# Branch outputs loaded straight into the low operand and split there, another planner's price for linear matmuls, and a beginning without GpSimd

## The chip, the cores and the metric

One core of one Trainium2 chip runs the whole layer in one launch. The metric is the device time of one execution in microseconds (us), the median of several executions. The kernel before takes 1955.33 us (median of three, 1954.95 to 1957.14).

## What is computed

The reference is one layer of a decoder trunk on x of 1024 positions by 1024 channels, all in float32. The gains, biases and norms are inputs.

```python
h = rms_norm(x, norm_g)
proj = einsum('bsd,dn->bsn', h, w_in)            # 11 blocks of 1024 columns, 16 gate columns, 3 x 1024 merge columns
ya = conformer_conv(a_val, a_glu, ...) * silu(a_gate)   # GLU, causal depthwise conv of width 31, LayerNorm, swish
yb = hgrn2(b_q, b_f, b_i, ...) * silu(b_gate)           # gated linear recurrence, 8 heads of 128
yc = forgetting_attention(c_q, c_k, c_v, ...) * silu(c_gate)  # 16 heads of 64, forget bias on the logits
branch_d = einsum('bskc,kcd->bskd', stack([ya, yb, yc]), w_branch)
mixed = sum(sigmoid(merge) * branch_d, over the three branches)
out = x + einsum('bsd,de->bse', mixed, w_out)
```

## The kernel before, in words

Everything is held transposed: channels on the 128 partitions, the 1024 positions along the free axis, in two halves of 512. A linear product is a "job" of 128 output columns (`Job`). Because the tensor engine's float32 product is taken in a rounded form (`F32R`), each operand is split into a high part (the rounded copy, made by ScalarE) and a low part (what is left, a subtraction on VectorE), and a job adds three products: high by high, low by high, high by low. A job so has 2 halves x 8 channel blocks x 3 = 48 matmuls of 128x128 by 128x512, all issued from L112 (`sc.mm`). Job 0 is narrow (the 16 forget gates) and has two products, 32 matmuls. `hT` holds the normed input (`hT_hi`, `hT_lo`), `whi` and `wlo` the weights of a job.

**Order.** `lin` (L352) walks the list of jobs; the first three go through their first halves, then through their second (`seq`). Everything else (the attention `att` and `soft`, the recurrence `hgrn`, the convolution `conv`, the loads `yload`) is a coroutine. `Sched.run` decides when a coroutine's next piece is emitted: it keeps a planned clock for each engine and lets a piece go when its planned ready time has been passed by TensorE's planned clock. Each linear matmul moves that clock by the number of ns given to `sc.mm`, 216 in L370 to L373. VectorE's long convolution is held near TensorE's planned clock in the same way. The order of emission is the priority from which a list scheduler then makes the final, fixed order of each engine and of each DMA queue; `tc.high_priority(HP)` lifts the instructions inside it by 300 places, and `tc.keep_in_program_order` (`K`, `pin`) ties an instruction behind the one before it on its engine.

**Stages.** (1) The beginning, L1200 to L1326: the eight blocks of 128 rows of x are loaded, `ident` is built (`make_identity`, GpSimd), 16 products of `ident` with itself (`NWARM`, L1215) run, each block is squared and summed by ScalarE (`x_sq`), its inverse root is refined on VectorE, the block is multiplied with `norm_g` (spread over all partitions in `gbc`) on VectorE or GpSimd, and it is transposed into `hT` by TensorE. The first four blocks are scaled inside the transposing product (`dgs`, L1269), the last four before it (L1254, L1258). GpSimd also makes `wlo` of jobs 1 and 2. (2) Eight rounds over channel blocks with the jobs of branches c and b. (3) The convolution stage, in which VectorE carries 31 taps for each of eight blocks and TensorE the jobs of branch c's output; it begins with `yload("c")`. (4) Branch b's outputs (after `yload("b")`), the gates of branch a, and the merge. (5) The last product with `w_out`, straight to the output.

**`yload` (L953)** brings a branch's output back from DRAM: for each of the eight channel blocks it takes one of the shared buffers `fa` (`F.get`, after `need(1)`), loads 512 KB into it, lets ScalarE make `Y["hi"][k]` and VectorE `Y["lo"][k]`, and gives the buffer back. `Y["hi"]` and `Y["lo"]` lie where the buffers of stage 2 (`fb`, queries, keys, gates) lay, opened by `swap` (L1151). VectorE and ScalarE take these instructions at the place where they were emitted. The jobs of the branch wait for `Y[b]`.

**`masks` (L294)** makes constants of the recurrence, by GpSimd (`affine_select`) and 16 small copies on ScalarE (L319 to L322).

Of the kernel before, what the change touches and what calls it, by code (L numbers as in the profile page):

```python
# [19 lines left out]
P = 128  # L20
# [27 lines left out]
PAD = 96  # L48
# [151 lines left out]
def build(tc, x, norm_g, w_in, conv_w, conv_b, ln_g, ln_b, hgrn_g, f_bias, qn_g, kn_g,  # L200
# [40 lines left out]
    make_identity(nc, ident)  # L241
# [14 lines left out]
    ones64 = const.tile([P, 64], F32, name="ones64")  # L256
    nc.vector.memset(ones64, 1.0)
# [11 lines left out]
    dgs = [const.tile([P, P], F32, name=f"dg{i}") for i in range(2)]  # L269
# [24 lines left out]
    def masks():  # L294
# [22 lines left out]
        for r in range(4):  # L317
            a = slice(r * 32, r * 32 + 32)
            nc.scalar.activation(cm[0][a, 0:32], ident[a, r * 32:r * 32 + 32], AF.Copy)  # L319
            nc.scalar.activation(cm[0][a, 32:48], lvl1[a, r * 16:r * 16 + 16], AF.Copy)  # L320
            for m in (2, 8):
                nc.scalar.activation(cm[m][a, :], lvl[m][a, r * 48:r * 48 + 48], AF.Copy)  # L322
# [29 lines left out]
    def lin(jobs, hooks):  # L352
        seq = [(0, 0), (1, 0), (2, 0), (0, 1), (1, 1), (2, 1)]
        seq += [(n, h) for n in range(3, len(jobs)) for h in (0, 1)]
        for m, (n, half) in enumerate(seq):
# [12 lines left out]
            for k in range(KT):  # L368
                a, b = X[0][k][:, hs], X[1][k][:, hs]
                sc.mm(ps, j.hi[:, k, :], a, k == 0, False, 216)  # L370
                sc.mm(ps, j.hi[:, k, :], b, False, j.narrow and k == KT - 1, 216)
                if not j.narrow:
                    sc.mm(ps, j.lo[:, k, :], a, False, k == KT - 1, 216)  # L373
                if k == 3:
                    yield 0
            if m in hooks:
                hooks[m]()
# [233 lines left out]
    def soft(st, i, T, MB, blks):  # L611
# [44 lines left out]
        for h in range(2):  # L656
            sc.mm(po[h * 64:(h + 1) * 64, 256:512], ones64, M[:, h, :], True, True, 225)
# [563 lines left out]
    def x_sq(i, pin):
        pin(nc.scalar.activation(sq[:, 0:S], xts[i][:, 0:S], AF.Square, accum_out=ss[:, i, 0:1]))

    def x_sqrt(i, pin):
        v, r, _ = col3(i)
        pin(nc.vector.tensor_scalar(out=v, in0=v, scalar1=1.0 / S, scalar2=EPS, op0=ALU.mult,
                                    op1=ALU.add))
        pin(nc.scalar.activation(r, v, AF.Sqrt))

    def x_g(i, pin):  # L1230
        e = nc.gpsimd if i % 2 else nc.vector
        pin(e.tensor_tensor(out=xg[i][:, 0:S], in0=xts[i][:, 0:S], in1=gbc[:, 0:S], op=ALU.mult))

    def x_newton(i, pin):
        v, r, e = col3(i)
        pin(nc.vector.reciprocal(r, r))
        pin(nc.vector.scalar_tensor_tensor(out=e, in0=r, scalar=v, in1=r, op0=ALU.mult,  # L1237
                                           op1=ALU.mult))
        pin(nc.vector.tensor_scalar(out=e, in0=e, scalar1=-0.5, scalar2=1.5, op0=ALU.mult,
                                    op1=ALU.add))  # L1240

    def x_dg(i, pin):
        v, r, e = col3(i)
        x_newton(i, pin)
        pin(nc.vector.tensor_scalar(out=dgs[i % 2], in0=ident, scalar1=r, scalar2=e,
                                    op0=ALU.mult, op1=ALU.mult))

    def x_rows(i, pin):

        v, r, e = col3(i)  # L1250
        xt = xg[i][:, 0:S]
        x_newton(i, pin)
        if i % 2:
            pin(nc.vector.tensor_scalar(out=xt, in0=xt, scalar1=r, scalar2=e, op0=ALU.mult,  # L1254
                                        op1=ALU.mult))
        else:
            pin(nc.vector.tensor_tensor(out=r, in0=r, in1=e, op=ALU.mult))
            pin(nc.vector.scalar_tensor_tensor(out=xt, in0=xts[i][:, 0:S], scalar=r,  # L1258
                                               in1=gbc[:, 0:S], op0=ALU.mult, op1=ALU.mult))

    def x_mm(i, pin):
        for hb in range(2):
            sbanks.append(sbanks.pop(0))
            pt = pts[i, hb] = sbanks[-1]
            for q in range(4):
                kk = hb * 4 + q
                o, a = pt[:, q * P:(q + 1) * P], xg[i][:, kk * P:(kk + 1) * P]
                if i < 4:
# [19 lines left out]
    def free(ins):  # L1288
        return ins
# [78 lines left out]
```

## Time and profile before

| | us |
|---|---|
| median of 3 runs | 1955.33 (1954.95 to 1957.14) |
| the profiled execution, whole | 1956.24 |
| its span, first to last instruction | 1954.5 |
| TensorE busy in the span | 1910.3 (98%) |
| VectorE, ScalarE, GpSimd busy | 1285.0, 956.5, 194.8 |
| mean granted clock of TensorE | 0.993 of full speed |

How to read it: the span is cut into stretches, and in each one looks first at what TensorE lacks to being busy and at the granted clock (1.00 is the 2.4 GHz level, 0.50 the 1.2 GHz level). A TensorE that is "busy" at half clock is counted as busy, so both columns are wanted. Then the list of waits says whom TensorE waited for, and the timeline shows the instructions around such a wait.

### The profile page before, as it was taken

To read this page: it belongs to the slowest core of one execution; us is meant where nothing else is said; L and a number is where in the kernel's file an instruction comes from. 1 tells how busy PE (TensorE), PEld (TensorE's weight loads), DVE (VectorE), ACT (ScalarE), POOL (GpSimd) and SP (SyncE) were. 2 spreads that over 40 slices of the span, in tenths; PEclk is the share of its full clock that TensorE was granted. 3 is DMA by queue.
4 is the path that set the end of the run, shared out by engine and by line. 5 is a ranking of instruction groups with operands and counts; after the bars stand their busy time and mean duration, and the time that the engine had idled before them with its cause. 6 is when DMAs were issued, how large, how long until landed. Compare 5 with 4: busy or idle time off the path is not lost.

```text
span 1954.5 us, 27130 instructions
## 1 busy us (share of the span) xinstructions
PE 1910.3 (98%) x11112; PEld 1550.0 (79%) x11112; DVE 1285.0 (66%) x1689; ACT 956.5 (49%) x1524; POOL 194.8 (10%) x157
## 2 busy tenths in 40 slices
PE   6999999999999999999999979999999999999999
PEld 5777877878778787787877857888888888888888
DVE  5357675676756867658677999999993367513431
ACT  5666868768687686776875231111131234312210
POOL 4011120211201211012021100000000110000000
PEclk9999999999999999999999989999999999999999
DMA  4111111111111111111112142222354553212431
GB/s 144 43 33 45 44 33 55 44 44 41 36 45 54 33 37 52 44 47 30 44 44 66 33 129 76 76 65 76 97 167 146 164 174 110 81 54 87 129 121 52
DMA packets 173140, 141.35 MB, mean 72 GB/s; under 512 B 4917, under 2 KB 155445, under 8 KB 173016
## 3 DMA queue, kind: packets, MB, share of 16 engines
q1 hardware_dynamic: 173016, 139.62, 23.2%
q8 instruction: 87, 1.43, 0.3%
q14 instruction: 37, 0.30, 0.1%
HBM read 110.24 MB, written 29.36 MB: 71 GB/s over the span
## 4 chain that ended last, share of the span: by engine, by line
PE 88%; DVE 5%; ACT 3%; issue 2%; DMA 1%; POOL 0%; DVEq 0%; SPq 0%; ACTq 0%; POOLq 0%
PE bank L112 86%; DVE fa L133 3%; PE bank L116 1%; ACT fb L125 1%; DMA zdram<-fa 1%; ACT fa L125 1%; DVE fa L129 1%; DVE wlo L348 1%; DMA fa<-zdram 1%; ACT khi L125 0%; DVE ylo L129 0%; DVE fb L129 0%; ACT whi L347 0%; DVE ss L1237 0%; PE bank L1271 0%
## 5 line engine op out<-in xcount | busy, mean ns | idle before, releaser
L112 PE MATMUL bank<-hT_hi,whi 128*128 128x512 f32 x1792 | 709.2, 396 | 3.2 <-ACT fb L125 1.5
L112 PE MATMUL bank<-hT_hi,wlo 128*128 128x512 f32 x1792 | 704.9, 394 | 0.4 <-DVE wlo L348 0.4
L112 PE MATMUL bank<-hT_lo,whi 128*128 128x512 f32 x1792 | 702.9, 392 | 0.0
L112 PEld LDWEIGHTS bank<-hT_hi,whi 128*128 128x128 f32 x1792 | 337.7, 188 | 77.9 <-issue 7.2
L112 PEld LDWEIGHTS bank<-hT_hi,wlo 128*128 128x128 f32 x1792 | 337.4, 188 | 76.1 <-issue 7.4
L112 PEld LDWEIGHTS bank<-hT_lo,whi 128*128 128x128 f32 x1792 | 337.8, 188 | 68.1 <-issue 3.8
L347 ACT ACTIVATE whi<-wraw 128x1024 fp32r<-128x1024 f32 x137 | 145.1, 1059 | 348.8 <-PE bank L112 334.3
L129 DVE TENSOR_TENSOR fa<-fa,fa 128x512 f32<-128x512 f32 (+3 forms) x299 | 236.5, 807 | 104.2 <-ACT fa L125 54.0
L133 DVE SCALAR_TENSOR_TENSOR fa<-fa,taps,fa 128x1024 f32<-128x1024 f32 x240 | 297.5, 1277 | 1.2
L348 DVE TENSOR_TENSOR wlo<-wraw,whi 128x1024 fp32r<-128x1024 f32 x135 | 171.9, 1273 | 162.5 <-ACT whi L347 162.2
L125 ACT ACTIVATE fa<-bank 128x512 f32<-128x512 f32 (+1 forms) x175 | 98.0, 565 | 170.4 <-PE bank L112 147.3
L112 PE MATMUL bank<-yhi,whi 128*128 128x512 f32 x384 | 150.8, 397 | 7.7 <-ACT yhi L125 7.7
L112 PE MATMUL bank<-ylo,whi 128*128 128x512 f32 x384 | 151.5, 395 | 6.2 <-DVE ylo L129 6.2
L125 ACT ACTIVATE fb<-bank 128x512 f32<-128x512 f32 (+6 forms) x269 | 121.2, 463 | 63.3 <-PE bank L112 36.9
L112 PE MATMUL bank<-yhi,wlo 128*128 128x512 f32 x384 | 150.7, 393 | 0.0
L129 DVE TENSOR_TENSOR fb<-fb,fb 128x512 f32<-128x512 f32 (+5 forms) x122 | 87.5, 733 | 33.1 <-ACT fb L125 29.3
L125 ACT ACT_TABLE_LOAD x83 | 106.5, 1283 | 5.1 <-DVE fb L129 3.6
L125 ACT ACTIVATE fa<-fa 128x1024 f32<-128x1024 f32 (+3 forms) x95 | 87.9, 940 | 39.3 <-DMA zdram<-fa 27.6
L133 DVE SCALAR_TENSOR_TENSOR fa<-fa,bank 128x512 f32<-128x512 f32 x82 | 56.0, 682 | 75.7 <-PE bank L112 75.7
L125 ACT ACTIVATE fa<-bank,negF,rk 128x256 f32<-128x256 f32 (+1 forms) x176 | 84.3, 549 | 38.4 <-PE bank L112 38.4
L125 ACT ACTIVATE fb<-fb 128x256 f32<-128x256 f32 (+5 forms) x105 | 77.1, 743 | 51.9 <-DVE fb L129 47.8
L112 PEld LDWEIGHTS bank<-yhi,whi 128*128 128x128 f32 x384 | 72.9, 191 | 24.3 <-ACT yhi L125 9.6
(200 smaller groups left out, 2097.3 us busy)
## 6 DMA issues: line engine op xcount, KB each, us to landing
wraw<-in_w_in_dram SPq DMA_DIRECT2D x113, 512.0 KB, 3.8
wraw<-in_w_branch_dram SPq DMA_DIRECT2D x24, 512.0 KB, 3.8
zdram<-fa SPq DMA_DIRECT2D x16, 512.0 KB, 2.7
mdram<-fa SPq DMA_DIRECT2D x32, 256.0 KB, 2.0
fa<-mdram SPq DMA_DIRECT2D x16, 512.0 KB, 4.4
fa<-zdram SPq DMA_DIRECT2D x16, 512.0 KB, 4.3
fa<-in_x_dram SPq DMA_DIRECT2D x9, 512.0 KB, 6.9
yb<-fb SPq DMA_DIRECT2D x8, 512.0 KB, 2.9
```

What stands on the lines that cost most here:

```text
L112: self.nc.tensor.matmul(out, lhsT=lhsT, rhs=rhs, start=start, stop=stop)
L116: self.nc.tensor.transpose(out, in_, ident)
L125: return self.nc.scalar.activation(out, in_, func, **kw)
L129: self.nc.vector.tensor_tensor(out=out, in0=a, in1=b, op=op)
L133: self.nc.vector.scalar_tensor_tensor(out=out, in0=a, scalar=s, in1=b, op0=op0, op1=op1)
L347: pin(nc.scalar.activation(j.hi, j.raw, AF.Copy))
L348: pin(eng.tensor_tensor(out=j.lo, in0=j.raw, in1=j.hi.bitcast(F32), op=ALU.subtract))
```

## The change

`ident` is now made without GpSimd: VectorE counts 1 to 128 along the free axis (a scan over ones), a product with one row turns the count into a column, and a comparison gives the identity. `norm_g` is no longer spread over the partitions: its 8 x 128 values are loaded from ScalarE's queue, transposed, and applied as a per-partition scale while the transposed blocks are taken out of PSUM (`gcol`). All eight blocks are scaled in place by VectorE and transposed. The first four blocks fill eight banks, one per channel block, so that one instruction per channel block and engine takes 512 columns out; the second four follow after the first, with hooks inside jobs 1 and 2 of `lin`. All `wlo` are made by VectorE. The five small loads of `gq`, `gk` and `fb` go from the sync queue to ScalarE's. The 16 small copies in `masks` go from ScalarE to GpSimd. `yload` loads all eight blocks straight into `Y["lo"]`, with no shared buffer, and then, at raised priority, copies each to `Y["hi"]` and subtracts in place. The planner's price of a linear matmul is 228 ns.

```diff
-PAD = 96
+PAD = 32
...
-    make_identity(nc, ident)
+    num = const.tile([P, P], F32, name="num")
+    ones64 = const.tile([P, P], F32, name="ones64")
+    nc.vector.memset(ones64, 1.0)
+    nc.vector.tensor_tensor_scan(out=num, data0=ones64, data1=ones64, initial=0.0, op0=ALU.mult,
+                                 op1=ALU.add)
+    nc.tensor.matmul(banks[6][:, 0:1], lhsT=num[0:1, :], rhs=ones64[0:1, 0:1], start=True, stop=True)
+    row_t = const.tile([P, 1], F32, name="row_t")
+    nc.vector.tensor_copy(row_t, banks[6][:, 0:1])
+    nc.vector.tensor_scalar(out=ident, in0=num, scalar1=row_t, scalar2=None, op0=ALU.is_equal)
...
-            nc.scalar.activation(cm[0][a, 0:32], ident[a, r * 32:r * 32 + 32], AF.Copy)
+            nc.gpsimd.tensor_copy(cm[0][a, 0:32], ident[a, r * 32:r * 32 + 32])
...
-                sc.mm(ps, j.hi[:, k, :], a, k == 0, False, 216)
+                sc.mm(ps, j.hi[:, k, :], a, k == 0, False, 228)
...
+                if (m, k) in hooks:
+                    hooks[m, k]()
                 if k == 3:
                     yield 0
-            if m in hooks:
-                hooks[m]()
...
         for k in range(KT):
-            yield need(1)
-            t = F.get()
-            nc.sync.dma_start(out=t[:, 0:S], in_=ydram[b][k])
-            sc.act(Y["hi"][k], t[:, 0:S], AF.Copy)
-            sc.tt(Y["lo"][k], t[:, 0:S], Y["hi"][k].bitcast(F32), ALU.subtract)
-            fput(t)
+            nc.sync.dma_start(out=Y["lo"][k].bitcast(F32), in_=ydram[b][k])
+        for k in range(KT):
+            with tc.high_priority(HP):
+                sc.act(Y["hi"][k], Y["lo"][k].bitcast(F32), AF.Copy)
+                sc.tt(Y["lo"][k], Y["lo"][k].bitcast(F32), Y["hi"][k].bitcast(F32), ALU.subtract)
             yield 0
...
+    nc.scalar.dma_start(out=g8, in_=norm_g.rearrange("a (k p) -> (a k) p", p=P))
+    for h in range(2):
+        for dst, a in ((gq, qn_g), (gk, kn_g)):
+            nc.scalar.dma_start(out=dst[h * 64:(h + 1) * 64, :], in_=a[0].unsqueeze(1))
+    nc.scalar.dma_start(out=fb, in_=f_bias[0].unsqueeze(1))
     for i in range(KT):
         nc.sync.dma_start(out=xts[i][:, 0:S], in_=x[i * P:(i + 1) * P, :])
-        if i == 0:
-            nc.sync.dma_start(out=gbc[:, 0:S], in_=norm_g.broadcast_to([P, S]))
-        if i in (3, 5, 7):
-            fetch(jobs[(i - 3) // 2])
+        if i in (3, 4, 7):
+            fetch(jobs[{3: 0, 4: 1, 7: 2}[i]])
...
+    def x_sq(i):
+        v, r = ss[:, i, 0:1], ss[:, i, 1:2]
+        K(nc.scalar.activation(sq[:, 0:S], xts[i][:, 0:S], AF.Square, accum_out=v))
+        K(nc.vector.tensor_scalar(out=v, in0=v, scalar1=1.0 / S, scalar2=EPS, op0=ALU.mult,
+                                  op1=ALU.add))
+        K(nc.scalar.activation(r, v, AF.Sqrt))
+
+    def x_rows(i):
...
+        K(nc.vector.tensor_scalar(out=xt, in0=xt, scalar1=r, scalar2=e, op0=ALU.mult, op1=ALU.mult))
...
+    def x_out(bk, k, half, pin=lambda ins: ins):
+        dst = [h[:, k, half * H2:(half + 1) * H2] for h in hT]
+        pin(nc.scalar.activation(dst[0], bk, AF.Copy, scale=gcol[:, k:k + 1]))
+        pin(nc.vector.scalar_tensor_tensor(out=dst[1], in0=bk, scalar=gcol[:, k:k + 1],
+                                           in1=dst[0].bitcast(F32), op0=ALU.mult, op1=ALU.subtract))
+
+    for i in range(4):
+        x_sq(i)
+        if i:
+            x_rows(i - 1)
+    x_rows(3)
+    for i in range(4):
+        for k in range(KT):
+            x_tr(banks[k], k, i, 0)
+    split(jobs[0], nc.vector, K)
     for k in range(KT):
+        x_out(banks[k], k, 0, K)
+        if k == 3:
+            split(jobs[1], nc.vector, K)
+    def x_second():
+        for i in range(4, KT):
+            x_sq(i)
+            if i > 4:
+                x_rows(i - 1)
+        x_rows(KT - 1)
+        split(jobs[2], nc.vector, K)
+
+    def x_two_out(g):
+        bk = xbanks[:4]
+        for i in range(4, KT):
+            for k in range(4):
+                x_tr(bk[k], 4 * g + k, i, 1)
+        for k in range(4):
+            x_out(bk[k], 4 * g + k, 1)
...
-    sc.run(lin(jobs, {0: lambda: x_two_out(4), 1: lambda: x_two_out(6)}))
+    sc.run(lin(jobs, {(1, 7): lambda: x_two_out(0), (2, 3): lambda: x_two_out(1)}))
```

## Rows read from the trace of the kernel before

**Rows 1.** Busy time by stretch: length, busy us of each engine, TensorE clock, DMA

```profile
0.00:48.86 48.86, 29.55 (x172) 25.89 (x173) 28.20 (x70) 27.09 (x63) 21.12 (x29) 0.96 0.44 144
...
146.59:195.45 48.86, 47.32 (x458) 35.13 (x458) 38.61 (x74) 31.33 (x59) 8.56 (x8) 1.00 0.15 45
...
830.66:879.52 48.86, 48.86 (x267) 42.20 (x267) 28.01 (x38) 36.02 (x55) 8.71 (x4) 1.00 0.16 47
...
1123.84:1172.70 48.86, 35.90 (x129) 26.46 (x128) 48.86 (x45) 15.37 (x16) 0.68 (x2) 0.81 0.40 129
...
1905.64:1954.50 48.86, 44.51 (x223) 39.92 (x221) 5.78 (x10) 0.00 (x0) 0.00 (x0) 0.99 0.13 52
```

**Rows 2.** Whom TensorE waited for: us in total, times, longest us

```profile
PE bank L1215 <- POOL ident masks.py:199: 12.3, 1, 12.3
PE bank L112 <- ACT yhi L125: 7.7, 3, 3.2
PE bank L112 <- DVE ylo L129: 6.2, 4, 2.0
```

**Rows 3.** Timeline of the beginning: start, length, engine, line, operation, idle before

```profile
11.92 0.28 POOL masks.py:199 TENSOR_SCALAR_AFFINE_SELECT ident<-ident 128x128 f32<-128x128 f32 x1 [10.50 <-issue]
...
13.20 1.06 ACT L1222 ACTIVATE fb<-fa 128x1024 f32<-128x1024 f32 x1
...
15.21 0.20 ACT L1228 ACTIVATE ss<-ss 128x1 f32<-128x1 f32 x1
...
27.99 0.47 PE L112 MATMUL bank<-hT_hi,fb 128*128 128x512 f32 x1
```

**Rows 4.** Groups by form, 0 to 60 us: busy, mean, idle before

```profile
L1277 DVE TENSOR_TENSOR hT_lo<-bank,hT_hi 128x512 fp32r<-128x512 f32 x16 | 10.3, 681 | 1.0 <-ACT hT_hi L1276 0.9
L1276 ACT ACTIVATE hT_hi<-bank 128x512 fp32r<-128x512 f32 x16 | 8.7, 602 | 3.2 <-PE bank L1271 1.8 <-DVE hT_lo L1277 1.1 <-PE bank L1269 0.3
...
L1237 DVE SCALAR_TENSOR_TENSOR ss<-ss 128x1 f32<-128x1 f32 x8 | 6.5, 814 | 0.2
```

**Rows 5.** Timeline from 39 us: GpSimd, VectorE, TensorE

```profile
41.03 2.35 POOL L1232 TENSOR_TENSOR fa<-fa,fa 128x1024 f32<-128x1024 f32 x1 [5.28 <-ACT fb L1222]
...
41.24 2.15 DVE L1237 SCALAR_TENSOR_TENSOR ss<-ss 128x1 f32<-128x1 f32 x1
...
45.76 1.11 PE L1271 MATMUL bank<-ident,fa 128*128 128x128 f32 x4 [4.99 <-DVE hT_lo L1277]
...
57.29 0.50 PE L112 MATMUL bank<-hT_hi,fb 128*128 128x512 f32 x1 [1.22 <-ACT hT_hi L1276]
```

**Rows 6.** Loads of x (line 1207), and a stretch of 10 us

```profile
DMA to landing us min/median/max: 3.7/6.9/9.8
...
10.00:20.00 10.00, 7.75 (x46) 7.75 (x47) 2.48 (x8) 6.50 (x23) 8.08 (x18) 1.00 0.90 308
```

**Rows 7.** Busy time around branch c's first job

```profile
1139.40:1179.53 40.13, 24.62 (x73) 16.06 (x72) 40.13 (x37) 10.07 (x10) 0.00 (x0) 0.74 0.36 118
1179.53:1240.00 60.47, 60.47 (x266) 49.81 (x267) 57.73 (x52) 8.85 (x12) 0.25 (x2) 1.00 0.28 87
```

**Rows 8.** Timeline, 1130 to 1190 us: store, copies, loads

```profile
1132.23 0.34 SPq L866 DMA_DIRECT2D yb<-fb  x1
...
1134.92 1.06 ACT L125 ACTIVATE yhi<-fa 128x1024 fp32r<-128x1024 f32 x1 [4.78 <-DVE wlo L348]
...
1138.64 1.21 DVE L129 TENSOR_TENSOR ylo<-fa,yhi 128x1024 fp32r<-128x1024 f32 x1
...
1139.88 2.16 SPq L959 DMA_DIRECT2D fa<-yc  x2
...
1147.06 22.15 SPq L959 DMA_DIRECT2D fa<-yc  x5
```

**Rows 9.** Convolution buffers: GpSimd clears one, VectorE fills it later

```profile
1280.95 0.12 POOL L879 MEMSET fa<- 128x30 f32 x1 [56.25 <-DVE fa L133]
...
1332.58 0.68 DVE L133 SCALAR_TENSOR_TENSOR fa<-fa,bank 128x512 f32<-128x512 f32 x1
```

More of the change, by code (lines that the diff above doesn't have):

```diff
@@ L6 @@
 from concourse import mybir
-from concourse.masks import make_identity
 F32 = mybir.dt.float32
@@ L268, in build @@
     ss = const.tile([P, KT, 4], F32, name="ss")
-    dgs = [const.tile([P, P], F32, name=f"dg{i}") for i in range(2)]
+    g8 = const.tile([KT, P], F32, name="g8")
+    gcol = const.tile([P, KT], F32, name="gcol")
     const.tile([P, PAD // 4], F32, name="pad")
@@ L1221, in x_sq @@
[L1221 to L1246, printed above, removed]
@@ L1261, in x_mm @@
[L1261 to L1268, printed above, removed]
-                    pin(nc.tensor.matmul(o, lhsT=a, rhs=dgs[i % 2], start=True, stop=True))
-                else:
-                    pin(nc.tensor.transpose(o, a, ident))
-    def x_out(i, hb, pin):
-        dst = [h[:, hb * 4:hb * 4 + 4, i * P:(i + 1) * P] for h in hT]
-        pv = pts[i, hb].rearrange("p (a b) -> p a b", a=4)
-        pin(nc.scalar.activation(dst[0], pv, AF.Copy))
-        pin(nc.vector.tensor_tensor(out=dst[1], in0=pv, in1=dst[0].bitcast(F32), op=ALU.subtract))
@@ L1295, in x_two_out @@
-    def x_two_out(i):
-        sbanks[:] = xbanks[:4]
-        for n in (i, i + 1):
-            x_mm(n, free)
-            for hb in range(2):
-                x_out(n, hb, free)
-        if i == 6:
-            fput(gbc, sq, *xts[4:])
-    split(jobs[1], nc.gpsimd, K)
-    x_two(4)
-    x_two(6)
-    split(jobs[2], nc.gpsimd, K)
+        if i in (3, 4, 7):
+            fetch(jobs[{3: 0, 4: 1, 7: 2}[i]])
     nc.sync.dma_start(out=vst[0:31, 0:S], in_=conv_w[0])
@@ L1320, in build @@
-    nc.vector.tensor_scalar(out=taps, in0=vecs[:, :, 0:31], scalar1=0.5, scalar2=None,
-                            op0=ALU.mult)
-    nc.vector.tensor_scalar(out=lnh, in0=vecs[:, :, 32:34], scalar1=0.5, scalar2=None,
-                            op0=ALU.mult)
-    nc.vector.tensor_scalar(out=ghalf, in0=vecs[:, :, 34:35], scalar1=0.5, scalar2=None,
-                            op0=ALU.mult)
-    fput(vst, *xgs, *xts[0:4])
+    for _ in range(NWARM):
+        nc.tensor.matmul(banks[7][:, 0:P], lhsT=ident, rhs=ident, start=True, stop=True)
@@ new lines, in build @@
+    nc.tensor.transpose(banks[6][:, 0:KT], g8, ident[0:KT, 0:KT])
+    nc.vector.tensor_copy(gcol, banks[6][:, 0:KT])
+    def x_sq(i):
[5 more added lines that the diff above has]
+    def x_rows(i):
+        v, r, e = (ss[:, i, n:n + 1] for n in range(3))
+        xt = xts[i][:, 0:S]
+        K(nc.vector.reciprocal(r, r))
+        K(nc.vector.scalar_tensor_tensor(out=e, in0=r, scalar=v, in1=r, op0=ALU.mult, op1=ALU.mult))
+        K(nc.vector.tensor_scalar(out=e, in0=e, scalar1=-0.5, scalar2=1.5, op0=ALU.mult,
+                                  op1=ALU.add))
+        K(nc.vector.tensor_scalar(out=xt, in0=xt, scalar1=r, scalar2=e, op0=ALU.mult, op1=ALU.mult))
@@ new lines, in x_two_out @@
+    def x_two_out(g):
[5 more added lines that the diff above has]
+            x_out(bk[k], 4 * g + k, 1)
+        if g == 1:
+            fput(sq, *xts[4:])
+            pt = xbanks[4]
+            for k in range(KT):
+                nc.tensor.transpose(pt[:, k * 35:(k + 1) * 35], vst[0:35, k * P:(k + 1) * P],
+                                    ident[0:35, 0:35])
+            nc.vector.tensor_copy(vecs, pt[:, 0:KT * 35].rearrange("p (k r) -> p k r", k=KT))
+            nc.vector.tensor_scalar(out=taps, in0=vecs[:, :, 0:31], scalar1=0.5, scalar2=None,
+                                    op0=ALU.mult)
+            nc.vector.tensor_scalar(out=lnh, in0=vecs[:, :, 32:34], scalar1=0.5, scalar2=None,
+                                    op0=ALU.mult)
+            nc.vector.tensor_scalar(out=ghalf, in0=vecs[:, :, 34:35], scalar1=0.5, scalar2=None,
+                                    op0=ALU.mult)
+            fput(vst)
@@ L1328, in build @@
+    x_second()
     masks()
```

60 lines of the change are left out of this document (10 added, 50 removed).

## The prediction

> **What bounds the kernel now.** I read the busy time first: TensorE is busy 1910.3 us of a span of 1954.5, so 44.2 us of idleness are all that waits alone can give back. By stretches of 48.86 us [rows 1] most of the run is full: the nineteen stretches from 195 to 1124 us are like the one at 830.66, 48.86 of 48.86 us busy at clock 1.00 (none lacks more than 0.3). The idleness lies in three places. The first stretch lacks 48.86 - 29.55 = 19.3 us; the stretch at 1123.84 lacks 13.0 us and its granted clock is 0.81, so part of its busy time is at the 1.2 GHz level; the last lacks 4.4 us, the tail after the last product, which the change leaves alone. Some 1.5 us lie in each of the first rounds (the stretch at 146.59). The waits name the causes [rows 2]: 12.3 us for `ident` from GpSimd, and 7.7 and 6.2 us for the high and low parts of branch c's outputs. The change goes at these places. The profiled execution took 1956.24 us, 0.9 us above the median of the runs; the sum is made against it.
>
> **The beginning.** What it removes: GpSimd stood 10.5 us before it built `ident` [rows 3], and ScalarE's first sum of squares (13.20 us) stood behind copies that need `ident`. The first linear matmul came at 27.99 us [rows 3], and job 0's second half began at 57.29 us [rows 5]. By then 16 + 24 + 24 = 64 linear matmuls were done, which at 60.47 us / 266 = 0.227 us each [rows 7] is 14.5 us of work in 29.3 us.
>
> What the new order costs, step by step. `ident` is now five small instructions on VectorE and TensorE; no row shows them in this order, so I bound them by 1 us (five of the 0.15 to 0.2 us that a small instruction takes) and 5 us (the same with a long handoff each); either is hidden, because the first x lands no earlier than 0.8 + 3.7 us [rows 6]. Four loads of x must land. A load takes 3.7 to 9.8 us, median 6.9 [rows 6], and the fourth is issued at about 3 us, so it lands at 8.5 to 11; I take 9.5. For the last of the four: 2.2 us from its square to its root (13.20 to 15.21 + 0.20, [rows 3]), about 1.5 us on VectorE for the refinement and the scaling (three small instructions with their handoffs and one over 1024 columns, estimated from the 0.68 us that 512 columns out of PSUM take, [rows 4]), 1 us of transposes (at half clock four took 1.11 us, [rows 5], so at full clock eight take about that), 0.6 us for the first copy out [rows 4]. First linear matmul: 9.5 + 5.3 = 14.8 us.
>
> The eight copies out are paced by VectorE: 8 x 0.68 [rows 4] + 1.2 for job 1's `wlo` = 6.7 us, so the 40 matmuls of the first halves of jobs 0 and 1 (9.1 us) end at about 24. Behind the eight copies and a split on ScalarE (14.2 + 8 x 0.6 + 1.1 = 20 us) stand in program order four sums of squares at 1.5 to 2.2 us each, ending at 26 to 29, then 1.5 us of scaling and 1.2 us for job 2's `wlo`: TensorE waits some 4 us for that, and job 2 starts at 29 to 32. With its 24 matmuls (5.5 us) and the transposes that are left (2 us) job 0's second half begins at 37 to 40; I take 39, against 57.29. From that I take 2 us off for the clock: the first stretch's 0.96 [rows 1] is some 4 us at the 1.2 GHz level, 2 us lost, and it stands where TensorE had waited 4.99 us, at 45.76 [rows 5]; the new order has such a wait too. Gain: 57.3 - 39 - 2 = 16 us, between 10 and 20.
>
> A price that speaks both ways: while GpSimd multiplied from 41.03 to 43.38 us, a VectorE instruction on 128x1 took 2.15 us [rows 5], and the eight of its kind average 814 ns [rows 4]. The change takes GpSimd's products away there, and puts 16 small copies on GpSimd behind its mask work, which now fall next to the copies out. The Trainium skill's page "SBUF — State Buffer", section "Who interferes with whom", says that a VectorE instruction with two SBUF inputs is blocked for the whole length of a GpSimd instruction that reads SBUF. The row agrees (2.15 against 2.35 us). By that rule the copies could add 1 or 2 us of blocking for the two `wlo`; without it, nothing. The bound of 10 us covers it.
>
> The five small loads moved to ScalarE's queue occupy that engine before the first x has landed; the sync queue loses them and a 512 KB spread load. The masks are needed first in the first recurrence, behind eight jobs of 48 x 0.227 = 10.9 us; those 87 us hide their move, and without them it would cost the copies' own time, some 16 x 0.2 us.
>
> **Branch c's outputs.** From 1139.40 to 1179.53 us TensorE did 73 matmuls [rows 7]: 48 of branch c's first job and 25 of the gates' job that fills in. At 0.227 us that is 16.6 us of work in 40.1 us: 23.5 us lost, 15.5 as idleness and the rest at a clock of 0.74. Why: the first copy went at 1134.92, 2.7 us after branch b's last store was issued [rows 8], which I take for the moment when the buffers of the old stage are free; loads two to eight were issued from 1139.88 to 1169, because each needed a shared buffer that the convolution also wanted [rows 8]; and the low part of block 0, ready to be made at 1136, was made at 1138.64, behind taps on VectorE, which was busy 40.13 of 40.13 us [rows 7].
>
> After: no buffer is needed, so eight loads can go from 1135 on. They are 4.19 MB; at the 308 GB/s of the loads at the start [rows 6] that is 13.6 us and some 2 us to complete: the last lands at 1151. Its copy (1.06) and subtraction (1.21 us) at raised priority end at 1153.5. Then block 7's three products and the second half are left, 27 x 0.227 = 6.1 us: 1160 us, while the filling job uses the waits before. Against 1179.53 that is 20 us; 3 us off for half clock during the waits and 2 for an order fixed on times a little other than the chip's: 15 us, between 5 (loads that share the queue and land as slowly as before, only the priority helping) and 22. Whom this makes wait: on the sync queue the eight loads stand in front of weight loads if the region is late; weights are fetched two jobs ahead, 22 us, so a wait of 5 us there is covered. On VectorE 8 x 1.21 us of taps move back by as much, which costs nothing as long as the convolution has slack: a buffer of it is cleared at 1280.95 and filled at 1332.58 [rows 9], 51 us. For branch b the loads can now start only when branch c's last job has read `Y["lo"]`; two gate jobs (22 us) stand between, against 16 + 2 us of loading, so I cost it at nothing.
>
> **The planner's price.** 0.227 us measured against 0.216 planned: side work is emitted some 5% fewer linear matmuls later. The rounds are full already, so at best the 3 us of idleness in the first rounds go; at worst (below) it costs. I take nothing, bounds -3 to +6.
>
> **Sum.** 1956.24 - 16 - 15 = 1925.2, less the 0.9 us between profile and median: 1924.5 us.
>
> **The rivals.** (1) The branch loads gain little: the region comes free late, or weights and loads share the queue, and TensorE still waits block by block. Gain there 3 to 5: 1924.5 + 11 = 1935.5. For it: loads took 3 to 4 us each with others in flight. Against: the shared buffer is plainly what spaced them. 13%. (2) The convolution takes the place of the wait: VectorE was full in that stretch and 57.73 of 60.47 us in the next [rows 7], TensorE comes 15 us earlier, and its results wait behind taps for a bank. It would give back up to 10 us: 1934. Against it: the 51 us [rows 9]. 10%. (3) The beginning does not get shorter as it says: four sums of squares in program order behind the copies leave TensorE starved and at half clock, job 0's second half at about 48: 1933. 8%. (4) Slower: the price of 228. With 216 each handoff from ScalarE or VectorE back to TensorE had 5% of slack that was not planned. If in the rounds each of some 15 handoffs in each of 8 rounds then waits 0.5 us, that is 60 us against 31 gained: 1985; it decides from 31 / 120 = 0.26 us a handoff on. For it: the first rounds, without backlog, have 1.5 us of idleness in a stretch [rows 1]. Against it: linear matmuls are nearly always there to fill, and rounds of the kind of 830.66 have no idleness at all [rows 1]. 7%. (5) Gains and losses of these kinds cancel: 1955, 3%.
>
> **How the numbers follow.** Forecast 59%, 1924.5, with its own range 1913 to 1933. With the three weaker gains (31%) the range that holds 8 in 10 is 1912 (both gains at their upper ends, 20 + 22 + 1) to 1941 (both at the lower, 10 + 5). A measurement of this kernel can tell about 0.2%, 4 us. Faster by more than that: 0.90; within: 0.03; slower: 0.07.
>
> **What would show it.** Right: first linear matmul at 13 to 16 us and job 0's second half near 39; the eight branch loads issued within 4 us of each other at about 1115 (all earlier by the first gain), the 73 matmuls there in some 25 us; rounds without idleness as before. Wrong: loads still spaced, new idleness of TensorE inside the rounds, waits for a bank behind taps between 1150 and 1400, or a longer stretch at half clock in the beginning than the 4 us of before.

## The result, and the profile after

The changed kernel takes 1909.32 us (median of four, 1908.57 to 1909.62) against 1956.24 of the kernel before on the same chip: ratio 0.9759, 95% interval 0.9742 to 0.9776. It gains 47 us; the forecast was 32, and the time lies 2.7 us below the range.

The page's busy time of each engine (share of the span, instructions), then the stretches that answer to [rows 1] (length, busy us of TensorE, its weight loads, VectorE, ScalarE, GpSimd; granted clock; DMA share, GB/s):

```profile
PE 1887.4 (99%) x11083; PEld 1551.7 (81%) x11083; DVE 1284.9 (67%) x1692; ACT 954.0 (50%) x1508; POOL 187.5 (10%) x164
```

```profile
0.00:48.86 48.86, 38.90 (x192) 32.94 (x193) 29.40 (x78) 27.78 (x52) 9.77 (x36) 0.93 0.45 143
...
830.66:879.52 48.86, 48.86 (x270) 40.73 (x270) 34.95 (x42) 37.62 (x61) 12.13 (x8) 1.00 0.19 54
1123.84:1172.70 48.86, 48.86 (x217) 40.46 (x216) 48.81 (x47) 7.48 (x9) 0.00 (x0) 1.00 0.25 77
```

Idleness fell from 44.2 to 20.5 us (span 1907.9). That is half of the gain; the other half, 22.9 us, is busy time of TensorE, which fell from 1910.3 to 1887.4 us. The stretch at 1123.84, which lacked 13.0 us at clock 0.81, is full at 1.00. The first still lacks 10.0 us and has a lower clock than before, 0.93. Whom TensorE waits for now (us in total, times, longest), where [rows 2] had `ident`, `yhi` and `ylo`:

```profile
PE bank L1246 <- DVE ss L1231: 3.2, 1, 3.2
PE bank L111 <- ACT fa L124: 2.6, 7, 0.4
PE bank L1223 <- DVE ident L249: 2.5, 1, 2.5
PE bank L115 <- ACT fb L124: 2.0, 7, 0.3
```

No wait of TensorE for branch c's outputs is left. Branch c's stores and loads, which answer to [rows 8] (timeline of SyncE's queue, 1041 to 1082 us):

```profile
1041.66 0.34 SPq L676 DMA_DIRECT2D yc<-fb  x1
1046.90 17.85 SPq L340 DMA_DIRECT2D wraw<-in_w_in_dram  x2
1072.97 3.72 SPq L964 DMA_DIRECT2D ylo<-yc  x8
1079.96 0.38 SPq L340 DMA_DIRECT2D wraw<-in_w_in_dram  x1
1081.83 0.32 SPq L873 DMA_DIRECT2D yb<-fa  x1
```

The loads go together, as forecast, but 42 us earlier than the 1115 us of the forecast, and ahead of branch b's last store, which [rows 8] have ahead of the copies. The first product with branch c's outputs starts at 1116.83, and the stretch that answers to [rows 7] is this:

```profile
1116.83:1133.00 16.17, 16.17 (x73) 13.40 (x72) 16.17 (x17) 2.10 (x2) 0.12 (x1) 1.00 0.29 99
```

73 matmuls took 40.13 us and now take 16.17, 24.0 less: all of the 23.5 us that the prediction counted as lost there have come back. 15.5 of the 24.0 are idleness (40.13 less 24.62 busy), the rest is busy time at a clock that was 0.74 and is 1.00.

The beginning, in place of [rows 3 to 5] (timeline: start, length, engine, line, operation, number, idle before and who ended it):

```profile
7.07 1.06 ACT L1230 ACTIVATE fb<-fa 128x1024 f32<-128x1024 f32 x1 [4.13 <-DMA gq<-in_fox_qn_g_dram]
...
11.15 0.23 PE L1224 MATMUL bank<-ident,g 8*128 8x8 f32 x1
11.41 0.17 DVE L1225 COPY gcol<-bank 128x8 f32<-128x8 f32 x1 [6.79 <-PE bank L1224]
11.50 0.14 DVE L1231 TENSOR_SCALAR ss<-ss 128x1 f32<-128x1 f32 x1
11.68 0.20 ACT L1233 ACTIVATE ss<-ss 128x1 f32<-128x1 f32 x1 [3.46 <-DVE ss L1231]
...
14.61 6.63 PE L1246 MATMUL bank<-ident,fa 128*128 128x128 f32 x32 [3.23 <-DVE ss L1231]
...
21.77 0.50 PE L111 MATMUL bank<-hT_hi,fb 128*128 128x512 f32 x1 [0.53 <-DVE hT_lo L1252]
```

`ident` is there at 4.6 us, but the first linear matmul starts at 21.77, not at 14.8. The first square was done at 8.1, and its root came at 11.68: VectorE, in order, stood at the copy of `gcol`, whose transpose stood behind the 16 warm products.

To see where time comes from I number the 6608 linear matmuls from 0 by their starts in the trace, and take for each kernel how much earlier than in the kernel before the n-th one starts. The 200th is behind the beginning, the 1200th behind the first rounds, the 3400th shortly ahead of branch c's first product (number 3488 in every kernel), the 3600th behind it.

| kernel | median us | ratio, 95% | 200 | 1200 | 3400 | 3600 | 5400 | end |
|---|---|---|---|---|---|---|---|---|
| whole change | 1909.32 | 0.9742 to 0.9776 | 13.2 | 21.7 | 22.5 | 46.8 | 46.8 | 46.7 |
| beginning alone | 1947.51 | 0.9938 to 0.9968 | 15.8 | 15.0 | 15.2 | 14.0 | 14.0 | 10.3 |
| loads alone | 1947.98 | 0.9940 to 0.9969 | 0.0 | -0.1 | -0.1 | 18.9 | 18.9 | 8.2 |
| price alone | 1927.01 | 0.9835 to 0.9864 | 0.0 | 8.0 | 8.6 | 32.9 | 27.4 | 28.1 |
| without the beginning | 1923.02 | 0.9810 to 0.9843 | -0.3 | 8.4 | 9.1 | 33.3 | 33.3 | 33.4 |
| without the loads | 1913.84 | 0.9764 to 0.9793 | 13.3 | 21.5 | 22.3 | 46.5 | 43.5 | 44.2 |
| without the price | 1936.23 | 0.9878 to 0.9911 | 14.6 | 13.9 | 14.1 | 32.7 | 32.7 | 20.0 |
| price 222 | 1922.50 | 0.9808 to 0.9837 | 14.5 | 13.6 | 13.7 | 32.4 | 32.4 | 33.1 |
| price 240 | 1915.18 | 0.9775 to 0.9804 | 13.6 | 17.3 | 20.1 | 44.3 | 43.1 | 39.8 |
| 228 up to two jobs ahead of branch c's first product | 1920.10 | 0.9795 to 0.9828 | 13.9 | 22.4 | 23.2 | 47.4 | 47.4 | 35.8 |
| 228 from two jobs ahead of branch c's first product | 1927.02 | 0.9830 to 0.9860 | 14.6 | 13.8 | 14.0 | 32.3 | 32.3 | 29.2 |
| 228 from the eighth round | 1925.53 | 0.9825 to 0.9858 | 15.6 | 14.8 | 15.0 | 33.4 | 33.4 | 32.1 |
| beginning mended | 1905.38 | 0.9726 to 0.9755 | 19.3 | 27.1 | 27.9 | 52.1 | 52.1 | 51.5 |

### The profile page after: what moved, and what is told of

The parts are those of the page before. It is cut to its first block, busy times and chain, and to the rows that moved or that the text cites. A ratio compares the mean times of both kernels' runs of the same rounds, so it can differ in the third digit from the quotient of the medians.

```text
span 1907.9 us, 27045 instructions
## 1 busy us (share of the span) xinstructions
PE 1887.4 (99%) x11083; PEld 1551.7 (81%) x11083; DVE 1284.9 (67%) x1692; ACT 954.0 (50%) x1508; POOL 187.5 (10%) x164
## 3 DMA queue, kind: packets, MB, share of 16 engines
q1 hardware_dynamic: 172520, 139.10, 23.5%
## 4 chain that ended last, share of the span: by engine, by line
PE 86%; ACT 8%; DVE 3%; DMA 2%; issue 1%; POOL 0%; DVEq 0%; SPq 0%; ACTq 0%; POOLq 0%
PE bank L111 84%; ACT fb L124 4%; ACT khi L124 2%; DVE fa L128 1%; PE bank L115 1%; DMA zdram<-fa 1%; ACT L124 1%; ACT fa L124 1%; DMA fa<-zdram 1%; ACT whi L354 0%; PE bank L1246 0%; PE bank L1223 0%; DVE wlo L355 0%; DVE fb L128 0%; DVE klo L132 0%
## 5 line engine op out<-in xcount | busy, mean ns | idle before, releaser
L355 DVE TENSOR_TENSOR wlo<-wraw,whi 128x1024 fp32r<-128x1024 f32 x137 | 191.6, 1399 | 126.4 <-ACT whi L354 125.6
L128 DVE TENSOR_TENSOR fa<-fa,fa 128x512 f32<-128x512 f32 (+3 forms) x226 | 173.4, 782 | 66.5 <-ACT fa L124 49.6
L124 ACT ACTIVATE fa<-bank 128x512 f32<-128x512 f32 (+1 forms) x182 | 103.3, 576 | 141.3 <-PE bank L111 128.1
L124 ACT ACTIVATE fb<-bank 128x512 f32<-128x512 f32 (+5 forms) x262 | 114.1, 450 | 41.2 <-PE bank L111 29.8
L128 DVE TENSOR_TENSOR fa<-fa,fb 128x512 f32<-128x512 f32 (+1 forms) x121 | 81.4, 672 | 58.9 <-ACT fb L124 37.8
L124 ACT ACTIVATE fb<-bank,negF,rk 128x256 f32<-128x256 f32 (+1 forms) x184 | 89.2, 549 | 49.1 <-PE bank L111 33.4
L132 DVE SCALAR_TENSOR_TENSOR fa<-fa,bank 128x512 f32<-128x512 f32 x96 | 65.4, 682 | 59.8 <-PE bank L111 59.7
L124 ACT ACTIVATE fa<-fa 128x256 f32<-128x256 f32 (+3 forms) x109 | 75.8, 720 | 53.4 <-DMA zdram<-fa 28.2
L124 ACT ACTIVATE fb<-fb 128x1024 f32<-128x1024 f32 (+2 forms) x96 | 88.1, 952 | 16.1 <-DVE fb L128 15.1
L111 PEld LDWEIGHTS bank<-yhi,wlo 128*128 128x128 f32 x384 | 72.1, 188 | 15.1
```

What stands on the lines that cost most here:

```text
L111: self.nc.tensor.matmul(out, lhsT=lhsT, rhs=rhs, start=start, stop=stop)
L124: return self.nc.scalar.activation(out, in_, func, **kw)
L128: self.nc.vector.tensor_tensor(out=out, in0=a, in1=b, op=op)
L132: self.nc.vector.scalar_tensor_tensor(out=out, in0=a, scalar=s, in1=b, op0=op0, op1=op1)
L355: pin(eng.tensor_tensor(out=j.lo, in0=j.raw, in1=j.hi.bitcast(F32), op=ALU.subtract))
```

## The experiments

**One part alone.** The first three runs are the kernel before with one part of the change each. Loads alone and beginning alone are the change's own lines for `yload` and for the beginning; the price alone is this:

```diff
-                sc.mm(ps, j.hi[:, k, :], a, k == 0, False, 216)
+                sc.mm(ps, j.hi[:, k, :], a, k == 0, False, 228)
...
-                    sc.mm(ps, j.lo[:, k, :], a, False, k == KT - 1, 216)
+                    sc.mm(ps, j.lo[:, k, :], a, False, k == KT - 1, 228)
```

> The kernel before with the planner's price of 228 alone. Theory A (three separate parts, read off the two traces at equal numbers of linear matmuls: beginning 13 us, first two rounds 8 us, branch c's outputs 24 us, each from its own edit): only the 8 us of the first rounds come, 1948 us, and TensorE still loses about 23 us at branch c's first job. Theory B (the price moves the last recurrence forward against the linear products, so that the old buffers come free before the jobs of branch c, and this rather than the form of the loads ends the wait): 8 + 15 to 20 us, 1928 to 1933, with the last store of branch b some 40 us behind the last store of branch c instead of 80.

> The kernel before with the new loads of the branch outputs alone (in place, raised priority). Theory A: the whole 24 us at branch c, 1932 us. Theory B: the region is still free only near 1135 us, so the loads start there and gain the 10 to 17 us of the prediction's sum: 1939 to 1946, with TensorE still waiting for branch c's parts.

> The kernel before with the new beginning alone. Both theories: 13 us by the 200th linear matmul, 1943 us, and waits at branch c as before.

The price alone, an edit in which no instruction differs but their order, gains 29.7 us, more than the other two together (9.3 and 8.8 by the medians): it is Theory B, by which the order frees the buffers early (1927.01 us, 1 us below its range). With the old loads, still spaced by the shared buffer, they simply have the time (timeline of SyncE's queue, price alone):

```profile
1055.53 0.34 SPq L669 DMA_DIRECT2D yc<-fb  x1
1058.77 0.34 SPq L959 DMA_DIRECT2D fa<-yc  x1
...
1094.96 0.32 SPq L866 DMA_DIRECT2D yb<-fa  x1
1097.29 2.07 SPq L959 DMA_DIRECT2D fa<-yc  x2
...
1116.67 0.32 SPq L959 DMA_DIRECT2D fa<-yc  x1
```

The first goes 3 us behind branch c's last store (in [rows 8], branch b's last store is at 1132.23) and the last at 1116.67, ahead of the first product at 1130.7. Loads alone do what the prediction said of them, at the time it said: here SyncE's queue in that kernel.

```profile
1132.35 0.34 SPq L866 DMA_DIRECT2D yb<-fb  x1
1134.68 0.37 SPq L333 DMA_DIRECT2D wraw<-in_w_in_dram  x1
1135.15 4.36 SPq L957 DMA_DIRECT2D ylo<-yc  x8
```

They gain 18.9 us at branch c (forecast 15), and 10.7 of it is lost again between the 5400th and the 5600th matmul, so the time, 1947.98 us, lies 2 us above Theory B's range. The beginning alone gains 15.8 us by the 200th matmul and 10.3 by the end, 1947.51 us where 1943 was expected. 3.7 us go at one place, the 5410th matmul: TensorE waits 2.46 us there for a `wlo`, 0.36 in the kernel before, and the granted clock is 0.50 from 1588.1 to 1591.6 us behind it.

**All but one part.** Each of the three is the changed kernel with one part put back.

> The changed kernel with the planner's price back at 216. Theory A: 1909 + 8 = 1917 us. Theory B: 1956 - 13 - (10 to 17) = 1926 to 1933 us, with waits for branch c's parts left.

> The changed kernel with the old loads (a shared buffer each, no priority). Theory A: 1909 + 24 = 1933 us, TensorE waiting for branch c's parts as before. Theory B: the region comes free early, so most of the wait is gone even with shared buffers: 1910 to 1918 us.

> The changed kernel with the old beginning. Both theories: 1909 + 13 = 1922 us; no wait for branch c's parts.

Without the price the change is worth 20.5 us (1936.23 us, 3 us above Theory B's range, for 12.7 us are given back late), without the loads 42.8 (Theory B), without the beginning 33.6. So the new loads carry 4.5 us beside the price by the medians (1913.84 against 1909.32, with intervals that overlap) and 2.5 by the two traces, none of it at branch c: the 3600th matmul stands at 46.5 without them and 46.8 with them. What they spare comes later: with the old loads 3.0 us are lost in branch b's products, where TensorE waits for the split of weights, 0.92 us for a `whi` at 1417 and 1.05 for a `wlo` at 1533; the price alone loses 5.5 us between the same marks, most of it at the same two matmuls (waits of 0.92 and 1.83 us, the second with the clock at 0.50 behind it). Why the split is late there was not looked for.

What gives time back without the price (the kernel without the price, timeline of VectorE and TensorE, 1601 to 1615 us):

```profile
1601.09 3.62 DVE L128 TENSOR_TENSOR fa<-fa,fa 128x1024 f32<-128x1024 f32 x3
1604.63 1.53 DVE L136 TENSOR_SCALAR fa<-fa,vecs 128x1024 f32<-128x1024 f32 x2
1606.08 1.22 DVE L132 SCALAR_TENSOR_TENSOR fa<-fa,fa 128x1024 f32<-128x1024 f32 x1
1607.21 1.22 DVE L355 TENSOR_TENSOR wlo<-wraw,whi 128x1024 fp32r<-128x1024 f32 x1
1608.35 3.49 DVE L132 SCALAR_TENSOR_TENSOR fa<-fa,fa 128x1024 f32<-128x1024 f32 x3
1611.75 1.22 DVE L128 TENSOR_TENSOR fa<-fa,fa 128x1024 f32<-128x1024 f32 x1
1612.89 1.22 DVE L128 TENSOR_TENSOR ylo<-fa,yhi 128x1024 fp32r<-128x1024 f32 x1
1614.02 1.28 DVE L132 SCALAR_TENSOR_TENSOR fa<-fa,bank 128x512 f32<-128x512 f32 x2
...
1614.76 0.80 PE L111 MATMUL bank<-hT_hi,whi 128*128 128x512 f32 x1 [10.43 <-DVE fa L132]
```

The emptying of a bank (`fa<-fa,bank`) stands in VectorE's queue behind some 13 us of other work, most of it the convolution's normalization. TensorE comes earlier by the whole gain and waits 10.43 us for a bank; the rest of the 12.7 us fits the granted clock, which is 0.50 from 1606.7 to 1620.4 us. In the kernel with the loads alone the wait is ahead of the same matmul, number 5576, and is 8.52 us long.

**The raised priority.** One run is the changed kernel without it, one the kernel before with it and nothing else:

```diff
-            with tc.high_priority(HP):
-                sc.act(Y["hi"][k], Y["lo"][k].bitcast(F32), AF.Copy)
-                sc.tt(Y["lo"][k], Y["lo"][k].bitcast(F32), Y["hi"][k].bitcast(F32), ALU.subtract)
+            sc.act(Y["hi"][k], Y["lo"][k].bitcast(F32), AF.Copy)
+            sc.tt(Y["lo"][k], Y["lo"][k].bitcast(F32), Y["hi"][k].bitcast(F32), ALU.subtract)
```

> The changed kernel with the loads in place but the split at its own place, not raised. If the early release is what counts, the split has 40 us before its first use and nothing changes: 1909 us. If the priority carries it, taps stand before the split and TensorE waits again: 1915 to 1925 us.

> The kernel before with raised priority on the split alone, loads through shared buffers as before. Under the prediction's reading (shared buffers space the loads) it gains only the waits behind taps, 3 to 6 us: 1950 to 1953 us.

Without it the changed kernel takes 1910.23 us (0.9746 to 0.9775), the kernel before with it alone 1956.04 (ratio 0.9996, 0.9987 to 1.0005), where 3 to 6 us of gain were expected. It decides nothing in either kernel.

**Where the price acts.** In the changed kernel, the price was set by the job, and then for all jobs to other values. The first of three kernels with two prices:

```diff
+            ns = 228 if n < NCUT else 216
...
-                sc.mm(ps, j.hi[:, k, :], a, k == 0, False, 228)
+                sc.mm(ps, j.hi[:, k, :], a, k == 0, False, ns)
```

`n` is the number of the job. The second kernel has 216 below `NCUT` and 228 from there on. In both, `NCUT` lies two jobs (96 linear matmuls) ahead of the first job with branch c's outputs, where the expectations have that job itself; in the first kernel branch b's last store is out by then. The third has 228 from the last job of the seventh round on.

> The changed kernel, 228 only for the jobs ahead of the first job that multiplies branch c's outputs, 216 from there to the end. Before, with 216 for all jobs (all but the price), the first 3400 linear matmuls gained 14.1 us, branch c 18.6 and 12.7 were given back at about 1604 us. Theory A, the price acts where it stands: the gain stands at 46 to 47 us at the 3600th matmul as with the whole change, and a wait of some 10 us comes back at about 1600: 1918 to 1922 us. Theory B, what is given back there is the debt of the first rounds' work, not of the later price: nothing is given back, 1908 to 1911 us.

> The changed kernel the other way round: 216 for the jobs ahead of the first that multiplies branch c's outputs, 228 from there on. Theory A, the price acts where it stands: 14.1 us at the 3400th matmul and 32.7 at the 3600th as with 216 for all jobs, but nothing is given back behind it: 1922 to 1926 us. Theory B, what is given back is the debt of the first rounds: the wait at about 1604 us stays and the time is that with 216 for all jobs, 1934 to 1938 us.

> The changed kernel with 216 for the jobs of the first seven rounds, 228 from the eighth round to the end. Theory A, what frees branch c's buffers early is the price in the last round alone, in which branch b's recurrence ends: nothing of the 5 to 7 us that the first rounds gained with 228, so some 14 us gained at the 3400th matmul, but no wait at branch c (38 at the 3600th) and nothing given back later: 1917 to 1921 us. Theory B, the recurrence must have been drawn forward from the first rounds on: 14 at the 3400th, branch c still waits for its loads (32 to 33 at the 3600th), 1923 to 1927 us as with 228 behind the rounds alone.

> The changed kernel with 222, half way between the old price of 216 (1936.2 us with the rest of the change) and 228 (1909.3). Theory A, the price brings its gain in proportion: about 1922 us. Theory B, it is a threshold, an order in which branch c's last store comes ahead of its buffers' use or not, and every price from some point below 227 on gives it: 1908 to 1912 us, or none of it, 1933 to 1937 us.

> The changed kernel with 240 ns as the price of a linear matmul where it has 228 (the trace's own spacing is 227 ns, 22.7 us for 100 matmuls). The order is fixed when the kernel is built, so a dearer matmul only means that more of the other engines' work is issued beside each job. Theory A, the price is right where it equals what a matmul takes: at 240 too much other work stands on VectorE between two evictions, TensorE waits for banks, some 3 to 25 us are lost, 1912 to 1935 us. Theory B, dearer is better as long as the recurrence is drawn forward: branch c still without a wait, no new waits, 1903 to 1909 us.

The early 228 gains all that the whole change does up to branch c (47.4), and the wait is back at 1600.27, 10.63 us long. The late 228 gains nothing ahead of branch c and loses 3.1 us instead of 12.7 behind it. So the price acts where it stands (Theory A of those two), though the second time, 1927.02 us, is 1 us above the range, which had nothing given back: the 3.1 us go at the 5410th matmul, as with the beginning alone (1.97 us for a `wlo`, then the clock at 0.50). The price from the eighth round on isn't enough: 33.4 us at the 3600th, Theory B. Nor is 222: its 1922.5 us are the number that went with a gain in proportion, but the marks show none of the price's gain up to branch c and all of it at 1600, where nothing is lost. 240 (1915.18 us, Theory A) is as good up to branch c within 2.5 us, with new waits in the rounds (six of 0.96 or 0.97 us for ScalarE's `fb`), and then loses 4.5, most of it in two waits (0.87 us at 1343, 2.10 at the 5410th matmul, the clock at 0.50 behind it). So at branch c and at 1600 us the price's gain is one order of the work or the other, and for branch c the order tips somewhere between 222 and 228. In the rounds 240 lies between (17.3 us at the 1200th, with 13.6 at 222 and 21.7 at 228).

What differs is this. VectorE's groups between branch c's last store and branch b's last, kernel before (80.0 us), then kernel after (40.2 us), costliest first:

```profile
L133 DVE SCALAR_TENSOR_TENSOR fa<-fa,taps,fa 128x1024 f32<-128x1024 f32 x40 | 50.0, 1278 | 0.3
L348 DVE TENSOR_TENSOR wlo<-wraw,whi 128x1024 fp32r<-128x1024 f32 x6 | 11.0, 1830 | 0.0
```

```profile
L132 DVE SCALAR_TENSOR_TENSOR fa<-fa,taps,fa 128x1024 f32<-128x1024 f32 x19 | 28.0, 1476 | 0.2
L355 DVE TENSOR_TENSOR wlo<-wraw,whi 128x1024 fp32r<-128x1024 f32 x3 | 3.7, 1218 | 0.0
```

And the end of the last recurrence in VectorE's queue, kernel before (timeline, 1110 to 1133 us):

```profile
1111.16 7.25 DVE L133 SCALAR_TENSOR_TENSOR fa<-fa,taps,fa 128x1024 f32<-128x1024 f32 x6
1118.34 0.74 DVE L133 SCALAR_TENSOR_TENSOR fb<-bank,ghalf,fb 128x512 f32<-128x512 f32 x1
1119.00 4.89 DVE L348 TENSOR_TENSOR wlo<-wraw,whi 128x1024 fp32r<-128x1024 f32 x1
1123.82 7.25 DVE L133 SCALAR_TENSOR_TENSOR fa<-fa,taps,fa 128x1024 f32<-128x1024 f32 x6
1130.99 1.21 DVE L129 TENSOR_TENSOR fb<-fb,fb 128x1024 f32<-128x1024 f32 x1
```

In VectorE's queue the recurrence that ends the old stage stood behind 40 taps of the convolution, twelve of them in its last 20 us, and with 228 it stands behind 19. In linear matmuls, branch b's last store comes at the 3457th in every kernel with 216 in the rounds, in the one with 228 from the eighth on and with 222, 31 ahead of branch c's first product; with 228 or 240 it comes at the 3331st to 3338th, 150 to 157 ahead. It goes with the price's gain at branch c in all of them. That a dearer matmul lets more side work be planned beside each job is how the planner is written; which of its decisions tipped was not looked for.

The 8 to 9 us in the rounds come with the price too (price alone, and the early 228), and they aren't idleness. When the 3400th linear matmul starts, the kernel before and the one with the price alone have both started the same 7512 matmuls, 3400 linear and 4112 others. TensorE had been idle for 24.0 us by then before and for 26.7 with the price alone; it had been busy for 1095.4 us and for 1084.2, and from 60 us on the granted clock is 1.00 in both. So in the new order the same matmuls take 11.3 us less of busy time; what shortens them was not looked for. Over the whole run (the pages of the kernel before and of the price alone, the same number of instructions):

```profile
PE 1910.3 (98%) x11112; PEld 1550.0 (79%) x11112; DVE 1285.0 (66%) x1689; ACT 956.5 (49%) x1524; POOL 194.8 (10%) x157
```

```profile
PE 1892.6 (98%) x11112; PEld 1554.9 (81%) x11112; DVE 1288.2 (67%) x1689; ACT 956.8 (50%) x1524; POOL 197.1 (10%) x157
```

Of the 28.1 us that the price alone gains by the two traces, 17.7 are busy time, most of them the 11.3 us of the rounds.

**A mended beginning.** The transpose of `norm_g` and its copy stand ahead of the warm products, and the five small loads go to SyncE's queue behind those of x:

```diff
-    for h in range(2):
-        for dst, a in ((gq, qn_g), (gk, kn_g)):
-            nc.scalar.dma_start(out=dst[h * 64:(h + 1) * 64, :], in_=a[0].unsqueeze(1))
-    nc.scalar.dma_start(out=fb, in_=f_bias[0].unsqueeze(1))
...
+    for h in range(2):
+        for dst, a in ((gq, qn_g), (gk, kn_g)):
+            nc.sync.dma_start(out=dst[h * 64:(h + 1) * 64, :], in_=a[0].unsqueeze(1))
+    nc.sync.dma_start(out=fb, in_=f_bias[0].unsqueeze(1))
+    nc.tensor.transpose(banks[6][:, 0:KT], g8, ident[0:KT, 0:KT])
+    nc.vector.tensor_copy(gcol, banks[6][:, 0:KT])
     for _ in range(NWARM):
         nc.tensor.matmul(banks[7][:, 0:P], lhsT=ident, rhs=ident, start=True, stop=True)
-    nc.tensor.transpose(banks[6][:, 0:KT], g8, ident[0:KT, 0:KT])
-    nc.vector.tensor_copy(gcol, banks[6][:, 0:KT])
```

> The changed kernel with its beginning mended at two places: the transpose of the norm's weights and its copy stand ahead of the warm products (in the changed kernel VectorE's copy waited behind them until 11.41 us and held up the first root), and six small loads issued by ScalarE (until 7.02 us, ahead of its first square at 7.07) are issued by SyncE behind the loads of x. Theory A, VectorE's order and ScalarE's issues held up the beginning: first square at about 5, transposes from about 11.2 without the 3.23 us of idle, first linear matmul at 16 to 18 us instead of 21.77, 1903 to 1906 us. Theory B, the loads of x or the half clock of the 32 transposes set it: first linear matmul at 20 to 21.8, 1907.5 to 1909.5 us.

1905.38 us, the best of all, with an interval (0.9726 to 0.9755) that reaches 0.0013 into the changed kernel's; the two were each timed against the kernel before. The first linear matmul starts at 15.55 us, and the gain at the 200th is 19.3 instead of 13.2: Theory A, a little earlier than its 16 to 18. The two places were mended in one run, so the share of each isn't shown. Its timeline of the beginning, then the stretch of the 32 transposes in the changed kernel and in this one (columns as in the first stretches above, the clock third from the end):

```profile
4.47 1.06 ACT L1230 ACTIVATE fb<-fa 128x1024 f32<-128x1024 f32 x1 [1.55 <-DMA fa<-in_x_dram]
...
11.09 3.66 PE L1246 MATMUL bank<-ident,fa 128*128 128x128 f32 x32
```

```profile
14.61:21.24 6.63, 6.63 (x32) 6.39 (x32) 4.42 (x16) 3.40 (x7) 6.13 (x23) 0.55 0.59 218
```

```profile
11.09:14.75 3.66, 3.66 (x34) 3.42 (x32) 2.32 (x7) 1.49 (x3) 2.74 (x9) 1.00 1.09 364
```

In the changed kernel TensorE was idle for 3.23 us ahead of the transposes and did them at clock 0.55, near the 1.2 GHz level. Here they follow the warm products without a gap, at 1.00, and take 3 us less.

## Why the prediction was wrong

**What bounds the kernel** was read in part. The idleness and the half clock at the two places of [rows 1] were there and came back. But the prediction took idleness and half clock for all that could be won, and so the rounds, full at clock 1.00, for a place that could give 3 us at most. Between the 200th and the 3400th matmul the whole change gains 9.3 us, all of it busy time at that clock (idleness grows by 2.2).

**The beginning, 16 us (10 to 20): near in size, 13.2, and wrong in a step.** The 2 us taken off for the clock were there (3 us, in the transposes). But the first linear matmul came 7 us later than the sum said, 3 of them for that clock and the rest for two things of program order that the diff shows and the sum left out. VectorE's copy of `gcol` stood behind the warm products, and the sentence that the five small loads occupy ScalarE "before the first x has landed" was false: they held it until 7.02 us, and in the mended kernel, without them, the first square starts at 4.47. With both put right the first linear matmul started at 15.55 us, 0.75 off the forecast: the sum of latencies was sound, the queues were not followed. Job 0's second half started at about 44 us, where the sum had 39 and 2 for the clock; that 7 us at the first matmul came to only 3 there was not foreseen. GpSimd's 16 copies ran from 17.77 to 22.2 us; the one low part that fell beside them took 0.28 us and job 1's came behind them, so nothing of the 1 or 2 us that could have come from there came.

**Branch c's outputs, 15 us (5 to 22): right for the edit, wrong for the kernel.** With 216 in the rounds the new loads gained 18.9 alone and 18.6 with the beginning, and they started at 1135 alone, where the sum had them. The shared buffer did space the old loads, but less because the convolution held it than because earlier blocks of the same branch did: of SyncE's waits ahead of these loads (kernel before, 1130 to 1175 us) 16.5 us end with a `ylo` subtraction, 7.2 with the landing of an earlier load and 1.4 with a tap. What was not seen is that 10.7 to 12.7 us of the gain are given back ahead of matmul 5576, at 1615 to 1627 us. This is rival (2) in kind (TensorE comes early, and an emptying of a bank waits behind VectorE's side work), at another place than between 1150 and 1400 us and with other work than taps. The 51 us of slack of [rows 9] didn't speak of that place.

**The planner's price, 0 (-3 to +6): this is the step that failed.** Alone it is worth 28 to 30 us. The reasoning took the price for a matter of side work moved by 5%, and looked for what it could win in the rounds, where no idleness was. It didn't ask what the order of the work decides: when the buffers of the old stage come free. That moment, read off [rows 8], was carried over into the forecast (1135, less the gain of the beginning) as if it belonged to the chip, though it belongs to the order, which this edit changes. In the changed kernel the loads start at 1072.97, and the whole 23.5 us come back with the old loads too. In the rounds themselves the price won 8 to 9 us of busy time, which the term had at nothing because there was no idleness. Rival (4) had the price as a loss of 0.26 us and more at each handoff: at 228 the list has fourteen such waits of at most 0.4 us, 4.6 us in all, and at 240 six of 0.96 or 0.97 us. The mechanism is there, below its point of 0.26 us a handoff on 120 handoffs.

**By the sum:** 13.2 at the beginning, 9.3 in the rounds, 24.3 at branch c, none given back: 47 measured, against 16 + 0 + 15. (1956.24 - 16 - 15 - 0.9 is 1924.3, not 1924.5; it changes nothing.) The terms don't add across edits: alone they bring 10.3 + 8.2 + 28.1 = 46.6 at the end, which comes near the 46.7 together only because two things cancel. Branch c's 23.5 us can be won once, by loads or by price (18.9 and 24.3 alone), and what each part alone gives back later is not given back by the whole: 10.7 us by the loads (the price in the late jobs ends that wait), 3.7 by the beginning and 5.5 by the price.

## What to carry to other kernels

Where the order of instructions is made by a planner with prices, a price is an edit to the whole order: ask what the order decides (when buffers come free, what an eviction stands behind), and don't bound it by the idleness of the stage where most of the priced work lies: the order changed the busy time as well. A start time read from the trace of before is the chip's only if nothing in the change moves what sets it. Judge a gain by how far it reaches: follow the same mark of progress to the end, for a queue further on may take it back.

## What the runs showed of the hardware

A VectorE instruction next to GpSimd's all-reduce is stretched (changed kernel, timeline, 1065 to 1072 us):

```profile
1065.64 6.12 POOL L869 PARTITION_ALL_REDUCE fb<-fa  x1 [0.61 <-ACT fa L124]
1066.25 5.01 DVE L132 SCALAR_TENSOR_TENSOR fa<-fa,taps,fa 128x1024 f32<-128x1024 f32 x1
```

The same tap takes 1.28 us elsewhere. The Trainium skill's page "SBUF — State Buffer", section "Who interferes with whom", says that a VectorE instruction with two inputs in SBUF contends with a GpSimd instruction that reads SBUF. The row agrees: 5.01 us for 1.28, though the tap ends at 1071.26, half a microsecond ahead of the all-reduce, so it was not held for its whole length. In the kernel before, the `wlo` at 1119.00 above took 4.89 us next to such an all-reduce (1118.14 to 1124.39), where others took 1.2. The 512 KB loads of the branches, issued eight in a row (branch c's within 3.72 us), took 7.2 to 8.9 us each to land (median 8.1), where the old, spaced ones took 3.1 to 4.4 (median 4.2); from 1072.97 to 1085.00 us the DMA engines moved 338 GB/s. GpSimd's first mask operation started at 12.75 us after 11.23 us in which it waited for nothing that the profile shows, much as in [rows 3], so that start was not `ident`'s own.
